# A two-layer conv / mLSTM / MLA block: 512-wide merges and a separate pool replaced by whole rows in generic slots, psum banks for the last chunk, and modulation pulled later

## The chip, the cores and the metric

The kernel runs on one core of one Trainium2 chip. The metric is the device time of one execution in microseconds; what is compared is the median of several runs.

## The reference

Two layers work on a sequence of 512 tokens and a context of 256 tokens, both 1024 wide. In each layer a modulation vector is made from `c` and `c_ctx`, one big projection `w_in` makes the inputs of three branches and their gates, the gated sum of the branches is projected and normalized, and an MLP with a squared ReLU follows. Cut to that:

```
mod = silu(c) @ w_mod[l] + b_mod[l]                 # six vectors of 1024; the same for c_ctx
u = x * (1 + sc1) + sh1
a, qkv, o_pre, g_if, cq, ckv, kr, gates = split(u @ w_in + b_in)
y_conv = silu(layer_norm(depthwise_conv(glu(a)))) @ w_conv_out
y_ml   = (sigmoid(o_pre) * layer_norm(mlstm(qkv, g_if))) @ w_mlstm_out
y_mla  = attention(cq, ckv, kr) @ w_mla_out         # keys of sequence and context
g_a, g_b, g_c = split(sigmoid(gates))
y = (g_a*y_conv + g_b*y_ml + g_c*y_mla) @ w_out + b_out
x = layer_norm(alpha*x + g1*y)
x = layer_norm(alpha*x + g2*(square(relu((x*(1+sc2)+sh2) @ w1 + b1)) @ w2 + b2))
```

In the first layer (layer 0) all of this is done for the context too. In the second (layer 1) the context only feeds attention and the mLSTM state, and the result is the sequence's `x`.

## The kernel before, in words

**Number format and weights.** Activations stand feature by token: a tile holds 128 features (partitions) and up to 768 tokens, 512 of the sequence and 256 of the context (`n` is 768 in layer 0, 512 in the later parts of layer 1; `segs` are these two pieces). Every product is made by three matmuls (`mm3`, L270 to L273) from a high and a low part of each factor. A weight tile of 128x1024 comes by a DMA on SP's queue (`wr`, L260), ScalarE casts it to the high part `wh` (L266), and VectorE or GpSimd subtracts to get the low part `wl` (L267). Three tiles of each exist, and `wget` loads two tiles ahead. `split` (L277, L278) does the same for an activation.

**Order of work.** A scheduler lays down a fixed order for each engine, and each engine works through its own in order; every DMA is issued on SP's queue. Only TensorE's order in the first stage and in the last chunk of layer 0 is written by hand (`manual_schedule`). TensorE's results go to psum: two tiles `pg` of two banks each and four tiles `pt` of one bank each. A tile of the next block may only be started when the operation that reads its predecessor is done.

**Modulation.** `mod_pieces` (L155 to L185) is a generator: a group of eight loads `wm` (256 KB each), eight or sixteen multiplies on VectorE into `mda` (L164, L166), eight small matmuls (L174), a copy (L177), a transpose (L179) and an add. There are four groups for each half of a layer's vectors. `pull(k)` lets the generator take k steps; it is called from the gates, the merges and the MLP, so the calls decide where these instructions stand.

**Gates, merges, output projection.** `gate` (L770) is a 128-row block of `w_in`, a tanh (L773), and a store to `z_dram`; there are 24 (three branches b of eight row blocks mt), then four O gates (L804) that stay in memory. Between the gates VectorE does the depthwise taps (L505), and after the eleventh gate the conv branch's LayerNorm stands (statistics, transposes L343 on TensorE, `conv_emit`). Then for each of the four mLSTM heads `ht` is transposed, multiplied by its O gate (L831), scaled (L832) and split (L277, L278). `merge(0)` multiplies the conv branch with `w_co`: eight blocks of twelve matmuls (three times 4) for each piece of tokens, and for each piece the gate is loaded again (`mload`, L77), multiplied with the psum tile (`ml`, L816) and stored. `merge(1)` does that for the mLSTM with `w_mo` and adds the sum so far. The MLA merge (L1091 to L1103) multiplies by `w_ao`, adds, and splits the total into `zp` (L1100 on ScalarE, L1101 on VectorE), the input of `w_out`. `mload` has eight tiles of 128x512 of its own (pool `mw`).

**Rows of constants.** `RC` holds five 1024-wide vectors; they are transposed (L853), stored to `v_dram`, and read back spread over 128 partitions by `rowv` (L858) into a pool `row` of five 128x1024 tiles. They are used in the MLP on GpSimd (L1252 to L1262) and, in layer 0, in the last chunk (L1274).

**MLP and the last chunk.** The MLP has eight chunks (`NF`) of 512 hidden features. In each, four blocks by `w1`, a squared ReLU, and `second`, which multiplies by `w2` token tile by token tile, for each half `hf` of the 1024 features, with VectorE adding the psum tile to `acc` (L1244). In the last chunk TensorE's order is by hand: for the four token tiles of the sequence (`GX`), then the two of the context (`GC`), half 0 and half 1 of the products; VectorE multiplies by a constant row into `t` (L1274) and adds (L1275); after half 1 the token's LayerNorm follows. The four tiles of `second` stand in the two `pg` tiles, one bank each, for both halves. After the context's products the sequence tokens are transposed (`tok_back`, L1191) and `norm2` (L1284 to L1294) makes the next layer's input: `xn` for a store, `uh` on ScalarE, `uf` on VectorE and `ul` on GpSimd, on VectorE for two of eight blocks.

**Pools.** Generic slots `gen` (128x768) 33; weights three each of `wr`, `wh`, `wl`; `mw` eight; `row` five.

Of the kernel before, what the change touches and what calls it, by code (L numbers as in the profile page):

```python
# [9 lines left out]
F32 = mybir.dt.float32  # L10
# [34 lines left out]
def build(tc, I, out):  # L45
    nc = tc.nc
# [1 line left out]
    ctx = ExitStack()  # L48
    cp = ctx.enter_context(tc.tile_pool(name="const", bufs=1))
    wp = ctx.enter_context(tc.tile_pool(name="w", bufs=3))  # L50
    gp = ctx.enter_context(tc.tile_pool(name="gen", bufs=33))
    vp = ctx.enter_context(tc.tile_pool(name="v", bufs=12))
    mp = ctx.enter_context(tc.tile_pool(name="mw", bufs=8))
    sp = ctx.enter_context(tc.tile_pool(name="small", bufs=6))
    pp = ctx.enter_context(tc.tile_pool(name="psum", bufs=1, space=bass.MemoryType.PSUM))
    rp = ctx.enter_context(tc.tile_pool(name="row", bufs=5))
    dp = ctx.enter_context(tc.tile_pool(name="dram", bufs=1, space=bass.MemoryType.DRAM))

    def slot(name, dt=F32):
# [13 lines left out]

    def mload(src):
        n = src.shape[1]
        t = mp.tile([128, 512], F32, name="ml", tag="m")
        nc.sync.dma_start(t[:, :n], src)  # L77
        return t[:, :n]

# [273 lines left out]
    def pull(k):  # L353
        for _ in range(k):
            next(mods, None)
# [108 lines left out]
    for l in range(L):  # L464
# [324 lines left out]
        for b in range(3):  # L789
            for mt in range(8):  # L790
                g = gate(b, mt)
                nc.sync.dma_start(z_dram[b, mt, :, :n], g[:, :n])
                some_taps(3)
                pull(2)
                if b * 8 + mt == 10:
                    some_taps(200)
                    ln_fm(ca, 4, groups, conv_emit)
# [3 lines left out]
        for h in range(MH):  # L801
            ps = win(MT_O + h, n)
            t = slot("ot")
            A.activation(t[:, :n], ps[:, :n], AF.Tanh, bias=HB(MT_O + h), scale=0.5)  # L804
            ot.append(t)
            pull(2)

        def merge(b, wname, act):
            for mp2 in range(4):
                w = wget(wname, l, mp2)  # L810
                for i in range(2):
                    mt = 2 * mp2 + i
                    ps = gemm(w, 4 * i, 4, act, n)
                    for c0, c1 in segs:
                        g = mload(z_dram[b, mt, :, c0:c1])
                        V.scalar_tensor_tensor(g, g, 1.0, ps[:, c0:c1], op0=OP.add, op1=OP.mult)  # L816
                        if b:
                            z0 = mload(z_dram[b - 1, mt, :, c0:c1])
                            G.tensor_tensor(g, g, z0, op=OP.add)
                        nc.sync.dma_start(z_dram[b, mt, :, c0:c1], g)  # L820
                    pull(2)


# [32 lines left out]
        nc.sync.dma_start(v_dram[l].rearrange("r (k j) -> (r k) j", j=128), rct[:40, :128])  # L856

        def rowv(i):  # L858
            t = rp.tile([128, 1024], F32, name="row", tag="row")
            nc.sync.dma_start(t, v_dram[l, i:i + 1, :].to_broadcast([128, 1024]))  # L860
            return t


        def latent(mt0, nt, gname, nn, scale):
# [225 lines left out]
        for mp2 in range(4):  # L1090
            w = wget("w_ao", l, mp2)  # L1091
            for i in range(2):
                mt = 2 * mp2 + i
                ps = gemm(w, 4 * i, 4, oT, n)
                for (_, _, c0, c1), zz in zip(tg_, zg):
                    g = mload(z_dram[2, mt, :, c0:c1])
                    z0 = mload(z_dram[1, mt, :, c0:c1])
                    V.scalar_tensor_tensor(g, g, 1.0, ps[:, c0:c1], op0=OP.add, op1=OP.mult)
                    V.tensor_tensor(g, g, z0, op=OP.add)
                    A.copy(zz[mt][0], g)  # L1100
                    V.tensor_sub(zz[mt][1], g, zz[mt][0])  # L1101

        u2 = [None] * 8  # L1103

# [92 lines left out]
        def second(f, hf, tts, wide):  # L1197

            ws = [None, None]
            sums = banks(len(tts), True) if wide else None  # L1200
            for i, tt in enumerate(tts):
                ps = sums[i] if wide else pt()
                for kp in range(2):
                    if not i:
                        ws[kp] = wget("w2", l, f, hf * 2 + kp)
                    tok_mm(ps, tt, hf, ws[kp], h_of, 2 * kp, 4)
                yield tt, ps
# [2 lines left out]
        b2r = [rowv(2 + v) for v in range(nv)]  # L1210
        g2r = [rowv(v) for v in range(nv)]
        if not full:
            folded.update({("w2", l, NF - 1, 2 * hf + kp): (g2r[0][:, hf * 512:hf * 512 + 512],)
                           for hf in range(2) for kp in range(2)})
        for f in range(NF):
            hid = []
            for j in range(FB):
                mt = f * FB + j
                last = j == FB - 1
                parts_f = split_spec if mt < 2 or last else [(c0, c1, c0) for c0, c1 in segs]  # L1220
                w = wget("w1", l, mt)
                if last:
                    sums = gemm_parts(w, 8, u2, parts_f)
                else:
                    sums = [(0, n, gemm(w, 0, 8, u2, parts_f)[:, :n])]
                r, hh, hl = slot("r"), slot("hidh", F32R), slot("hidl", F32R)
                for c0, c1, ps in sums:
                    A.activation(r[:, c0:c1], ps, AF.Relu, bias=col(l, "b1", mt))
                    A.activation(hh[:, c0:c1], r[:, c0:c1], AF.Square)
                    V.tensor_tensor(r[:, c0:c1], r[:, c0:c1], r[:, c0:c1], op=OP.mult)  # L1230
                    V.tensor_sub(hl[:, c0:c1], r[:, c0:c1], hh[:, c0:c1])  # L1231
                pull(1)
                hid.append((hh, hl))
            def h_of(k, tt):
                return hid[k][0][:, tt * 128:tt * 128 + 128], hid[k][1][:, tt * 128:tt * 128 + 128]

            if f < NF - 1:
                for hf in range(2):
                    for tt, ps in second(f, hf, qts, False):
                        if f == 0:  # L1240
                            acc[tt, hf] = vt512("acc")
                            A.copy(acc[tt, hf], ps)
                        else:
                            V.tensor_tensor(acc[tt, hf], acc[tt, hf], ps, op=OP.add)  # L1244
                        if tt % 3 == 2:
                            pull(1)
            if 1 <= f <= 6:
                for tt, hf in [(tt, hf) for tt in qts for hf in range(2)][2 * (f - 1):2 * f]:
                    r = wtile("r2")
                    o = hf * 512  # L1250
                    nc.sync.dma_start(r, n_dram[tt, hf])
                    G.tensor_tensor(r, r, a2r[:, o:o + 512], op=OP.mult)  # L1252
                    G.tensor_tensor(r, r, b2r[kind(tt)][:, o:o + 512], op=OP.add)
                    nc.sync.dma_start(r_dram[tt, hf], r)
            if f == 6:
                for hf in range(2):
                    for tt in qts:
                        o = hf * 512
                        r = wtile("r2")
                        nc.sync.dma_start(r, r_dram[tt, hf])  # L1260
                        G.tensor_tensor(acc[tt, hf], acc[tt, hf], g2r[kind(tt)][:, o:o + 512], op=OP.mult)
                        G.tensor_tensor(acc[tt, hf], acc[tt, hf], r, op=OP.add)  # L1262
        pull(99)
        if full:
# [2 lines left out]


        def last_w2(tts, hf):
            for tt, ps in second(NF - 1, hf, tts, True):  # L1270
                t = ps
                if full:
                    t = wtile("t2")
                    V.tensor_tensor(t, ps, g2r[kind(tt)][:, hf * 512:hf * 512 + 512], op=OP.mult)  # L1274
                V.tensor_tensor(acc[tt, hf], acc[tt, hf], t, op=OP.add)  # L1275
                tok_stats(tt, hf, acc[tt, hf])
                if hf:
                    yield tt

        if full:  # L1280
            u = [None] * 8

            def norm2(k, c0, c1, ps):
                v = 0 if c0 < S else 1  # L1284
                if c0 == 0:
                    u[k] = (slot("uh", F32R), slot("ul", F32R))
                if v == 0:
                    xn = wtile("xn")
                    A.activation(xn[:, :c1 - c0], ps, AF.Identity, bias=col(l, "ln2_b", k), scale=col(l, "ln2_g", k))
                    nc.sync.dma_start(xs_dram[k, :, c0:c1], xn[:, :c1 - c0])  # L1290
                uf = slot("uf")
                A.activation(u[k][0][:, c0:c1], ps, AF.Identity, bias=nq_[:, k, v:v + 1], scale=np_[:, k, v:v + 1])  # L1292
                V.tensor_scalar(uf[:, c0:c1], ps, np_[:, k, v:v + 1], nq_[:, k, v:v + 1], op0=OP.mult, op1=OP.add)
                (V if k % 4 == 3 else G).tensor_sub(u[k][1][:, c0:c1], uf[:, c0:c1], u[k][0][:, c0:c1])  # L1294

            with tc.manual_schedule(engines={mybir.EngineType.PE}):
                for gi, tts in enumerate((GX, GC)):
# [125 lines left out]
```

## Time and profile before

| | |
|---|---|
| median of 3 runs | 2570.15 us (2569.47 to 2571.76) |
| the profiled execution | 2566.69 us, of which the span of the trace is 2564.9 us |
| mean granted TensorE clock | 0.989 |
| TensorE (PE) busy | 2463.4 us, 96% of the span, 14618 matmuls |
| weight loads (PEld) busy | 2130.0 us, 83%, beside the matmuls |
| VectorE (DVE) busy | 1586.3 us, 62% |
| ScalarE (ACT) busy | 928.5 us, 36% |
| GpSimd (POOL) busy | 419.7 us, 16% |
| moved by DMA | 319.40 MB |

A row of a timeline gives the start in us from the span's start, the duration, the engine, the line, the operation, output<-inputs, the shape, and how many such instructions stand in a row; the bracket behind it says how long the engine was idle before it and what ended that. In the row of a group the times of all its instructions are added. In the list of DMA issues the last number is the median time from issue to landing.

### The profile page before, as it was taken

The page shows a single profiled execution, that of the slowest core. Times are in us where ns is not written, and L with a number is a line of the kernel's source. Part 1 is how long each engine was busy: PE and PEld are TensorE (multiplying, and loading weights), DVE is VectorE, ACT ScalarE, POOL GpSimd, SP SyncE. Part 2 cuts the span into 40 slices and gives each one's busy share as a digit, 9 for nine tenths or more (in the row PEclk, how much of TensorE's full clock was granted, in tenths as well). Part 3 has the DMA queues.
Part 4 walks back from the last instruction along what each step waited for, and adds up shares of the span by engine and source line. Part 5 has one row for each costly group of instructions (what it writes and reads, how often), then busy time and mean ns, then how long its engine had stood idle before and what let it go on. Part 6 is the DMA issues. An engine that isn't in the chain of part 4 may idle for free.

```text
span 2564.9 us, 37165 instructions
## 1 busy us (share of the span) xinstructions
PE 2463.4 (96%) x14618; PEld 2130.0 (83%) x14618; DVE 1586.3 (62%) x2795; ACT 928.5 (36%) x1577; POOL 419.7 (16%) x319
## 2 busy tenths in 40 slices
PE   7899989999999999999999979999999999999997
PEld 5888868888887898888888858978888889888886
DVE  4999976363356776655555379996043567544447
ACT  3123323222457553222222243333324575432322
POOL 0002132202000030010011520024421001500025
PEclk9999999999999999999999999999999999999999
DMA  7122344567110664444444232233563107633332
GB/s 263 53 75 69 101 159 160 172 198 241 62 33 5 195 204 144 128 145 139 147 131 140 80 97 82 65 107 97 177 211 127 50 18 230 206 98 91 106 91 83
DMA packets 148852, 319.40 MB, mean 125 GB/s; under 512 B 15076, under 2 KB 56628, under 8 KB 148676
## 3 DMA queue, kind: packets, MB, share of 16 engines
q1 hardware_dynamic: 148676, 317.02, 38.5%
q8 instruction: 115, 1.88, 0.3%
q14 instruction: 61, 0.50, 0.1%
HBM read 275.97 MB, written 40.98 MB: 124 GB/s over the span
## 4 chain that ended last, share of the span: by engine, by line
PE 50%; DVE 7%; issue 2%; ACT 2%; POOL 1%; DMA 0%; POOLq 0%; DVEq 0%; ACTq 0%
PE pg L271 8%; PE pg L272 8%; PE pg L273 8%; PE pt L272 6%; PE pt L273 6%; PE pt L271 6%; DVE ca L505 2%; DVE wl L267 1%; PE pt L1040 1%; PE pt L1019 1%; ACT wh L266 1%; PE pg L549 0%; PE pg L551 0%; PE pg L550 0%; DVE r L1230 0%
## 5 line engine op out<-in xcount | busy, mean ns | idle before, releaser
L266 ACT CAST wh<-wr 128x1024 fp32r<-128x1024 f32 (+2 forms) x320 | 337.6, 1056 | 1137.0 <-PE pg L272 493.1
L267 DVE TENSOR_TENSOR wl<-wr,wh 128x1024 fp32r<-128x1024 f32 (+1 forms) x264 | 344.8, 1307 | 448.0 <-ACT wh L266 447.2
L271 PE MATMUL pg<-uh,wh 128*128 128x512 f32 (+1 forms) x1280 | 456.9, 357 | 3.0 <-ACT uh L1292 1.8
L273 PE MATMUL pg<-uh,wl 128*128 128x512 f32 (+1 forms) x1280 | 454.9, 355 | 2.2 <-DVE wl L267 2.2
L272 PE MATMUL pg<-ul,wh 128*128 128x512 f32 (+1 forms) x1280 | 454.9, 355 | 0.6 <-POOL ul L1294 0.6
L271 PEld LDWEIGHTS pg<-uh,wh 128*128 128x128 f32 x1280 | 243.8, 191 | 38.3 <-issue 2.5
L273 PEld LDWEIGHTS pg<-uh,wl 128*128 128x128 f32 x1280 | 243.6, 190 | 34.9 <-DVE wl L267 2.7
L272 PEld LDWEIGHTS pg<-ul,wh 128*128 128x128 f32 x1280 | 244.0, 191 | 33.4 <-POOL ul L1294 1.6
L267 POOL TENSOR_TENSOR wl<-wr,wh 128x1024 fp32r<-128x1024 f32 x56 | 146.7, 2619 | 537.3 <-ACT wh L266 537.3
L505 DVE SCALAR_TENSOR_TENSOR ca<-hc,cols,ca 128x511 f32<-128x511 f32 (+9 forms) x360 | 227.1, 671 | 2.3
L273 PE MATMUL pt<-wh,hidl 128*128 128x512 f32 x560 | 218.7, 391 | 1.8 <-DVE hidl L1231 1.8
L272 PE MATMUL pt<-wl,hidh 128*128 128x512 f32 x560 | 219.0, 391 | 0.6 <-DVE wl L267 0.6
L271 PE MATMUL pt<-wh,hidh 128*128 128x512 f32 x560 | 218.4, 392 | 0.0
L272 PE MATMUL pg<-u2l,wh 128*128 128x512 f32 (+1 forms) x608 | 211.3, 348 | 0.6 <-POOL u2l L1112 0.2
L271 PE MATMUL pg<-u2h,wh 128*128 128x512 f32 (+1 forms) x608 | 210.4, 347 | 0.0
L273 PE MATMUL pg<-u2h,wl 128*128 128x512 f32 (+1 forms) x608 | 209.9, 346 | 0.0
L166 DVE SCALAR_TENSOR_TENSOR mda<-wm,sil,mda 128x512 f32<-128x512 f32 x224 | 180.0, 824 | 6.9 <-DMA wm<-w_mod 4.2
L1244 DVE TENSOR_TENSOR acc<-acc,pt 128x512 f32<-128x512 f32 x120 | 82.1, 684 | 123.0 <-PE pt L273 122.8
L272 PEld LDWEIGHTS pg<-u2l,wh 128*128 128x128 f32 x608 | 115.2, 189 | 17.1 <-POOL u2l L1112 2.6
L271 PEld LDWEIGHTS pg<-u2h,wh 128*128 128x128 f32 x608 | 115.0, 189 | 15.3 <-issue 1.2
L273 PEld LDWEIGHTS pg<-u2h,wl 128*128 128x128 f32 x608 | 115.0, 189 | 14.0
L273 PEld LDWEIGHTS pt<-wh,hidl 128*128 128x128 f32 x560 | 105.6, 188 | 24.7 <-DVE hidl L1231 2.6
(387 smaller groups left out, 4908.1 us busy)
## 6 DMA issues: line engine op xcount, KB each, us to landing
wr<-w SPq DMA_DIRECT2D x132, 512.0 KB, 3.5
wr<-w_in_fm SPq DMA_DIRECT2D x104, 512.0 KB, 3.6
wm<-w_mod SPq DMA_DIRECT2D x192, 256.0 KB, 4.3
wr<-w_out SPq DMA_DIRECT2D x40, 512.0 KB, 4.2
ml<-z_dram SPq DMA_DIRECT2D x104, 128.0 KB, 2.7
ml<-z_dram SPq DMA_DIRECT2D x48, 256.0 KB, 4.2
z_dram<-ml SPq DMA_DIRECT2D x32, 256.0 KB, 3.4
dm<-m_dram SPq DMA_DIRECT2D x20, 256.0 KB, 4.4
```

The source lines that it names most:

```text
L166: ins = V.scalar_tensor_tensor(av[v], w, sil[:, k, v:v + 1], av[v], op0=OP.mult, op1=OP.add)
L266: A.copy(h[:, :n], r[:, :n])
L267: eng.tensor_sub(lo[:, :n], r[:, :n], h[:, :n])
L271: PE.matmul(ps, hs, xh, start=first, stop=False)
L272: PE.matmul(ps, hs, xl, start=False, stop=False)
L273: return PE.matmul(ps, ls, xh, start=False, stop=last)
L505: V.scalar_tensor_tensor(acc[:, a:b], h[:, a + d:b + d], wd(15 + d), acc[:, a:b], op0=OP.mult, op1=OP.add)
L1019: PE.transpose(p2[:, y * 128:(y + 1) * 128], P[:, (k4 + y) * 128:(k4 + y + 1) * 128], ident)
L1040: PE.matmul(po[64 * i:64 * i + 64, :256], va[B_.k0 + k][:, h * 64:h * 64 + 64], B_.pts[i][k // 2][:, k % 2, :], start=(k == 0), stop=(k == ...
L1244: V.tensor_tensor(acc[tt, hf], acc[tt, hf], ps, op=OP.add)
```

## The change

1. The pool `gen` grows from 33 to 40 slots. The pool `row` goes: `rowv` now loads each row as two halves of 512 into generic slots. The loads of `mload` take a generic slot too; the pool `mw` is kept.
2. The gates call `pull(3)`, but only for the second and third branch (from the ninth gate on), where all called `pull(2)`; the O gates call `pull(3)`.
3. The merges work on whole rows of `n` tokens: one load, one multiply, one add, one store for a row block where layer 0 had two of each. In the MLA merge the total is split by groups afterwards.
4. In the last chunk `second` takes banks by `wide`: half 0 of the four sequence tokens in the two `pg` tiles as before, half 1 in the four `pt` tiles; the two context tokens stay in `pg`. Before, all stood in `pg`. In the second layer the same holds for its four tokens.
5. In `norm2` the last subtract is always on GpSimd.

The core of the diff:

```diff
-    gp = ctx.enter_context(tc.tile_pool(name="gen", bufs=33))
+    gp = ctx.enter_context(tc.tile_pool(name="gen", bufs=40))
-    rp = ctx.enter_context(tc.tile_pool(name="row", bufs=5))
...
-        t = mp.tile([128, 512], F32, name="ml", tag="m")
+        t = slot("ml")
...
-                pull(2)
+                if b:
+                    pull(3)
...
             ot.append(t)
-            pull(2)
+            pull(3)
...
                     ps = gemm(w, 4 * i, 4, act, n)
-                    for c0, c1 in segs:
-                        g = mload(z_dram[b, mt, :, c0:c1])
-                        V.scalar_tensor_tensor(g, g, 1.0, ps[:, c0:c1], op0=OP.add, op1=OP.mult)
-                        if b:
-                            z0 = mload(z_dram[b - 1, mt, :, c0:c1])
-                            G.tensor_tensor(g, g, z0, op=OP.add)
-                        nc.sync.dma_start(z_dram[b, mt, :, c0:c1], g)
+                    g = mload(z_dram[b, mt, :, :n])
+                    V.scalar_tensor_tensor(g, g, 1.0, ps[:, :n], op0=OP.add, op1=OP.mult)
+                    if b:
+                        z0 = mload(z_dram[b - 1, mt, :, :n])
+                        G.tensor_tensor(g, g, z0, op=OP.add)
+                    nc.sync.dma_start(z_dram[b, mt, :, :n], g)
...
-            t = rp.tile([128, 1024], F32, name="row", tag="row")
-            nc.sync.dma_start(t, v_dram[l, i:i + 1, :].to_broadcast([128, 1024]))
-            return t
+            ts = [slot("row")[:, :512] for _ in range(2)]
+            for hf, t in enumerate(ts):
+                nc.sync.dma_start(t, v_dram[l, i:i + 1, hf * 512:hf * 512 + 512].to_broadcast([128, 512]))
+            return ts
...
                 ps = gemm(w, 4 * i, 4, oT, n)
+                g = mload(z_dram[2, mt, :, :n])
+                z0 = mload(z_dram[1, mt, :, :n])
+                V.scalar_tensor_tensor(g, g, 1.0, ps[:, :n], op0=OP.add, op1=OP.mult)
+                V.tensor_tensor(g, g, z0, op=OP.add)
                 for (_, _, c0, c1), zz in zip(tg_, zg):
-                    g = mload(z_dram[2, mt, :, c0:c1])
-                    z0 = mload(z_dram[1, mt, :, c0:c1])
-                    V.scalar_tensor_tensor(g, g, 1.0, ps[:, c0:c1], op0=OP.add, op1=OP.mult)
-                    V.tensor_tensor(g, g, z0, op=OP.add)
-                    A.copy(zz[mt][0], g)
-                    V.tensor_sub(zz[mt][1], g, zz[mt][0])
+                    A.copy(zz[mt][0], g[:, c0:c1])
+                    V.tensor_sub(zz[mt][1], g[:, c0:c1], zz[mt][0])
...
-            sums = banks(len(tts), True) if wide else None
+            sums = banks(len(tts), wide) if f == NF - 1 else None
...
-            for tt, ps in second(NF - 1, hf, tts, True):
+            for tt, ps in second(NF - 1, hf, tts, len(tts) == 2 or not hf):
...
-                (V if k % 4 == 3 else G).tensor_sub(u[k][1][:, c0:c1], uf[:, c0:c1], u[k][0][:, c0:c1])
+                G.tensor_sub(u[k][1][:, c0:c1], uf[:, c0:c1], u[k][0][:, c0:c1])
```

The edits move instructions in the order of the engines. Three places follow, each as it stood before and as it stands now; after the change the lines of the helpers and of the gates and merges have a number lower by one (L174 becomes L173, L267 L266, L278 L277, L816 L815, L831 L830, L832 L831).

**TensorE, gates of layer 0.** Here is the first group of modulation matmuls (`mda`, L174) in TensorE's order. Before, it stands in a gate's block (`pg<-uh,wh`), some three gates ahead of the conv's LayerNorm:

```order
L271 MATMUL pg<-uh,wh 128x512
L272 MATMUL pg<-ul,wh 128x512
L174 MATMUL pt<-mda,pick 32x128 x4
L273 MATMUL pg<-uh,wl 128x512
L174 MATMUL pt<-mda,pick 32x128 x4
L271 MATMUL pg<-uh,wh 128x512
L272 MATMUL pg<-ul,wh 128x512
L179 MATMUL pt<-cst,modrows 128x128
L273 MATMUL pg<-uh,wl 128x512
```

Now it stands in the last gate ahead of the LayerNorm's transposes (`cst,ca`, L318):

```order
L270 MATMUL pg<-uh,wh 128x512
L271 MATMUL pg<-ul,wh 128x512
L173 MATMUL pt<-mda,pick 32x128 x8
L272 MATMUL pg<-uh,wl 128x512
L270 MATMUL pg<-uh,wh 128x512
L178 MATMUL pt<-cst,modrows 128x128
L318 MATMUL pt<-cst,ca 128x128 x16
```

All eight matmuls (L173) now stand together, and 16 transposes follow at the end of the same gate.

**VectorE, the start of the conv merge in layer 1.** `ht` is the mLSTM head's output, `htl` its low part, `ml` the merge's row, `wl` the low part of a merge's weights. Before, the merge's multiplies (L816) alternate with the heads:

```order
L816 SCALAR_TENSOR_TENSOR ml<-ml,pg 128x512
L267 TENSOR_TENSOR wl<-wr,wh 128x1024
L278 TENSOR_TENSOR htl<-ht,hth 128x512
L831 SCALAR_TENSOR_TENSOR ht<-ot,pt 128x512
L816 SCALAR_TENSOR_TENSOR ml<-ml,pg 128x512
L832 TENSOR_SCALAR ht<-ht,cols_86 128x512
L278 TENSOR_TENSOR htl<-ht,hth 128x512
L831 SCALAR_TENSOR_TENSOR ht<-ot,pt 128x512
L816 SCALAR_TENSOR_TENSOR ml<-ml,pg 128x512
L832 TENSOR_SCALAR ht<-ht,cols_86 128x512
L267 TENSOR_TENSOR wl<-wr,wh 128x1024
```

Now the heads' operations come first, and four multiplies (L815) follow together:

```order
L266 TENSOR_TENSOR wl<-wr,wh 128x1024
L277 TENSOR_TENSOR htl<-ht,hth 128x512
L830 SCALAR_TENSOR_TENSOR ht<-ot,pt 128x512
L831 TENSOR_SCALAR ht<-ht,cols_83 128x512
L277 TENSOR_TENSOR htl<-ht,hth 128x512
L830 SCALAR_TENSOR_TENSOR ht<-ot,pt 128x512
L831 TENSOR_SCALAR ht<-ht,cols_83 128x512
L277 TENSOR_TENSOR htl<-ht,hth 128x512
L815 SCALAR_TENSOR_TENSOR ml<-ml,pg 128x512 x4
L266 TENSOR_TENSOR wl<-wr,wh 128x1024
```

The first L815 in this order now stands behind the last `htl` (L277).

**VectorE and SP, the MLA merge in layer 1.** On VectorE the multiply (L1098 before, L1097 now), the add (L1099, now L1098) and the split (L1101) of one row block, before in two halves of 256 tokens:

```order
L1098 SCALAR_TENSOR_TENSOR ml<-ml,pg 128x256
L267 TENSOR_TENSOR wl<-wr,wh 128x1024
L1101 TENSOR_TENSOR zp<-ml,zp 128x256
L1099 TENSOR_TENSOR ml<-ml 128x256
L1098 SCALAR_TENSOR_TENSOR ml<-ml,pg 128x256 x2
L1101 TENSOR_TENSOR zp<-ml,zp 128x256
L1099 TENSOR_TENSOR ml<-ml 128x256 x2
L1101 TENSOR_TENSOR zp<-ml,zp 128x256
L1098 SCALAR_TENSOR_TENSOR ml<-ml,pg 128x256
L1101 TENSOR_TENSOR zp<-ml,zp 128x256
L267 TENSOR_TENSOR wl<-wr,wh 128x1024
```

and now in one of 512:

```order
L266 TENSOR_TENSOR wl<-wr,wh 128x1024
L1097 SCALAR_TENSOR_TENSOR ml<-ml,pg 128x512
L1098 TENSOR_TENSOR ml<-ml 128x512
L1097 SCALAR_TENSOR_TENSOR ml<-ml,pg 128x512
L1101 TENSOR_TENSOR zp<-ml,zp 128x256 x2
L1098 TENSOR_TENSOR ml<-ml 128x512
L1101 TENSOR_TENSOR zp<-ml,zp 128x256 x2
L1097 SCALAR_TENSOR_TENSOR ml<-ml,pg 128x512
L1098 TENSOR_TENSOR ml<-ml 128x512
L266 TENSOR_TENSOR wl<-wr,wh 128x1024
```

The low part of the weights (`wl`) now stands ahead of two multiplies in a row of L1097 and L1098, where halves of L1098 and L1101 stood around it. On SP's queue, before, the loads of the gates' rows (L77) stand in halves between the loads of the weights (L260):

```order
L77 DMA ml<-z_dram 128x256 x14
L260 DMA wr<-w_out 128x1024
L77 DMA ml<-z_dram 128x256 x7
L260 DMA wr<-w_out 128x1024
L77 DMA ml<-z_dram 128x256 x8
L260 DMA wr<-w_out 128x1024
L77 DMA ml<-z_dram 128x256 x3
L1120 DMA xr<-xs_dram 128x2x256 x4
L260 DMA wr<-w_out 128x1024
```

and now in whole rows (L76) between the weights (L259), with the loads of the block input (`xr`) further ahead:

```order
L76 DMA ml<-z_dram 128x512 x2
L1120 DMA xr<-xs_dram 128x2x256 x3
L76 DMA ml<-z_dram 128x512 x2
L259 DMA wr<-w_out 128x1024
L76 DMA ml<-z_dram 128x512 x4
L259 DMA wr<-w_out 128x1024
L76 DMA ml<-z_dram 128x512 x2
L259 DMA wr<-w_out 128x1024
L76 DMA ml<-z_dram 128x512 x6
L259 DMA wr<-w_out 128x1024 x9
```

There are 32 loads of halves in the stretch shown before, and 16 of whole rows now.

More of the change, by code (lines that the diff above doesn't have):

```diff
@@ L1199, in second @@
             ws = [None, None]
-            sums = banks(len(tts), True) if wide else None
+            sums = banks(len(tts), wide) if f == NF - 1 else None
             for i, tt in enumerate(tts):
-                ps = sums[i] if wide else pt()
+                ps = sums[i] if sums else pt()
                 for kp in range(2):
@@ L1212, in build @@
         if not full:
-            folded.update({("w2", l, NF - 1, 2 * hf + kp): (g2r[0][:, hf * 512:hf * 512 + 512],)
+            folded.update({("w2", l, NF - 1, 2 * hf + kp): (g2r[0][hf],)
                            for hf in range(2) for kp in range(2)})
@@ L1251, in build @@
                     nc.sync.dma_start(r, n_dram[tt, hf])
-                    G.tensor_tensor(r, r, a2r[:, o:o + 512], op=OP.mult)
-                    G.tensor_tensor(r, r, b2r[kind(tt)][:, o:o + 512], op=OP.add)
+                    G.tensor_tensor(r, r, a2r[hf], op=OP.mult)
+                    G.tensor_tensor(r, r, b2r[kind(tt)][hf], op=OP.add)
                     nc.sync.dma_start(r_dram[tt, hf], r)
@@ L1260, in build @@
                         nc.sync.dma_start(r, r_dram[tt, hf])
-                        G.tensor_tensor(acc[tt, hf], acc[tt, hf], g2r[kind(tt)][:, o:o + 512], op=OP.mult)
+                        G.tensor_tensor(acc[tt, hf], acc[tt, hf], g2r[kind(tt)][hf], op=OP.mult)
                         G.tensor_tensor(acc[tt, hf], acc[tt, hf], r, op=OP.add)
@@ L1273, in last_w2 @@
                     t = wtile("t2")
-                    V.tensor_tensor(t, ps, g2r[kind(tt)][:, hf * 512:hf * 512 + 512], op=OP.mult)
+                    V.tensor_tensor(t, ps, g2r[kind(tt)][hf], op=OP.mult)
                 V.tensor_tensor(acc[tt, hf], acc[tt, hf], t, op=OP.add)
```

## The prediction

> **What bounds the kernel now.** I read the page first, then what TensorE (PE) waited for over the whole run, then the table of windows for the clock, then the timelines around the places that the diff touches. The page shows one engine that is nearly always busy:
>
> ```profile
> span 2564.9 us, 37165 instructions
> PE 2463.4 (96%) x14618; PEld 2130.0 (83%) x14618; DVE 1586.3 (62%) x2795; ACT 928.5 (36%) x1577; POOL 419.7 (16%) x319
> ```
>
> PE is idle for about 101 us. The change adds and removes no matmul, so it can only move PE's waits and its clock. The list of PE's waits (total, times, longest, in us) has these that stand where the diff is:
>
> ```profile
> PE pt L174 <- DVE mda L166: 9.7, 2, 8.0
> PE pg L271 <- DVE t L1274: 7.1, 6, 2.0
> PE pt L343 <- ACT ln L331: 6.0, 9, 2.2
> PE pt L1191 <- DVE uf L1293: 5.0, 3, 2.8
> PE pg L271 <- DVE acc L1275: 3.6, 2, 3.0
> PE pg L271 <- DVE ml L816: 1.7, 1, 1.7
> PE pg L271 <- DVE ml L1098: 1.0, 2, 0.8
> ```
>
> The merges (L816, L1098) cost almost nothing now. A wait also has a second price, in the table of windows of 3.41 us (length, PE busy, granted clock):
>
> ```profile
> 331.50:334.94 3.44, 0.00 (x0) 1.00 0.65 251
> 338.35:341.77 3.42, 3.42 (x19) 0.50 0.81 244
> ...
> 1502.30:1505.71 3.41, 1.44 (x8) 1.00 0.52 159
> 1505.71:1509.12 3.41, 3.41 (x8) 0.50 0.39 149
> ```
>
> After 1.97 us of idleness in one window, the next window, fully busy, was granted 0.50: a loss of half of it, 1.7 us. The Trainium skill (TensorE: Matmul & The Clock Gate, HAM oscillation — how this bites in real kernels) asks only that no gap be longer than about 3.4 us; the trace disagrees, with 1.97. By that rule the clock costs that I add to the two output-projection merges (3.6 in all) would be nil and the 1.7 won back in the last chunk too, and the sum 1.9 lower.
>
> **Gates of layer 0.**
>
> ```profile
> 337.78 0.66 PE L174 MATMUL pt<-mda,pick 128*32 128x128 f32 x8 [7.98 <-DVE mda L166]
> ...
> 331.69 6.70 DVE L166 SCALAR_TENSOR_TENSOR mda<-wm,sil,mda 128x512 f32<-128x512 f32 x10
> ...
> 374.37 2.93 DVE L166 SCALAR_TENSOR_TENSOR mda<-wm,sil,mda 128x512 f32<-128x512 f32 x1
> ...
> wm<-w_mod SPq DMA_DIRECT2D x192, 256.0 KB, 4.3
> ```
>
> The first modulation group now stands directly ahead of the conv's LayerNorm transposes, some three gates later. The 7.98 us go, and with them the half clock from 337.78 to 341.77 (half of 4.0, 2.0 us). The multiply that took 2.93 us between the LayerNorm's statistics stands no longer there, so most of the 2.2 us wait on L331 goes: 2.0. What is late next: the sixteen multiplies need eight loads, five of which stand on SP behind the store of the ninth gate. From that store PE has two gates of 8.34 us (spacing of the casts below) to go; loads 4.3, five issues and the last two multiplies make about 7.5. No wait. The second group keeps a wait of 1.7 (14 multiplies instead of 4 are left when the LayerNorm is done, 6.7 us more, but PE comes about 7 us later). Sum -12.0; bounds -8 (LayerNorm waits stay, 2 us for late loads) and -14.
>
> **Last chunk of layer 0.**
>
> ```profile
> 1490.82 0.50 PE L271 MATMUL pg<-wh,hidh 128*128 128x512 f32 x1 [1.25 <-DVE t L1274]
> 1497.93 0.50 PE L271 MATMUL pg<-wh,hidh 128*128 128x512 f32 x1 [1.37 <-DVE t L1274]
> ...
> 1505.64 0.76 PE L271 MATMUL pg<-wh,hidh 128*128 128x512 f32 x1 [1.97 <-DVE t L1274]
> ```
>
> The second half of the four sequence tokens gets four single banks, so the first two waits (2.6) go. The third was for tiles held by that half; about 1.0 stays between the halves of one tile, 1.0 goes, and the half-clock window after it, 1.7. PE then reaches the transposes L1191 3.6 us earlier and waits there for the same `uf`: I let 1.0 be lost, moving the last `ul` to GpSimd included. Sum -4.3; bounds -1 and -9 (the half-clock windows there go too).
>
> **Merge of the conv branch, layer 1.** New: all DVE work on `ht` stands ahead of the first L815, the operation that frees a psum tile, where it alternated before. PE has two tiles, so the third block waits.
>
> ```profile
> 1883.27 0.69 DVE L816 SCALAR_TENSOR_TENSOR ml<-ml,pg 128x512 f32<-128x512 f32 x1 [0.19 <-PE pg L273]
> 1886.89 1.23 DVE L267 TENSOR_TENSOR wl<-wr,wh 128x1024 fp32r<-128x1024 f32 x1 [0.22 <-ACT wh L266]
> 1888.03 0.69 DVE L278 TENSOR_TENSOR htl<-ht,hth 128x512 fp32r<-128x512 f32 x1
> 1888.63 0.68 DVE L831 SCALAR_TENSOR_TENSOR ht<-ot,pt 128x512 f32<-128x512 f32 x1
> 1889.83 0.48 DVE L832 TENSOR_SCALAR ht<-ht,cols 128x512 f32<-128x512 f32 x1
> ...
> 1880.36 1.05 ACT L266 CAST wh<-wr 128x1024 fp32r<-128x1024 f32 x1 [3.80 <-issue]
> 1885.80 1.05 ACT L266 CAST wh<-wr 128x1024 fp32r<-128x1024 f32 x1 [2.08 <-PE pg L272]
> 1890.40 0.62 ACT L277 CAST hth<-ht 128x512 fp32r<-128x512 f32 x1 [3.02 <-DVE ht L832]
> ```
>
> Both casts at 1880.36 and 1885.80 start as PE frees weights: two blocks take 5.44 us. At 1885.8 the second is done, and the third needs L815, which stands behind this chain from 1888.03: `htl` 0.60, `ht` 0.60 and 0.48, `hth` 0.62, `htl` 0.60, again 0.60, 0.48, 0.62, 0.60, then L815 0.69 and some hand-offs: 1894.1. PE is ready at 1886.2, after the row transpose that now comes first: it waits 7.9, bounds 6 and 9. Clock afterwards 1.7 (0.8 to 2.6, by where the restart falls in a window). Sum +9.6.
>
> **The same, layer 0.**
>
> ```profile
> 530.86 1.05 ACT L266 CAST wh<-wr 128x1024 fp32r<-128x1024 f32 x1 [6.49 <-issue]
> 542.65 1.05 ACT L266 CAST wh<-wr 128x1024 fp32r<-128x1024 f32 x1
> ...
> 531.38 1.02 DVE L831 SCALAR_TENSOR_TENSOR ht<-ot,pt 128x512 f32<-128x512 f32 x2 [5.10 <-PE pt L829]
> 533.45 0.61 DVE L832 TENSOR_SCALAR ht<-ht,cols 128x768 f32<-128x768 f32 x1
> 534.96 0.96 DVE L278 TENSOR_TENSOR htl<-ht,hth 128x768 fp32r<-128x768 f32 x1 [0.90 <-ACT hth L277]
> ...
> 534.10 0.83 ACT L277 CAST hth<-ht 128x768 fp32r<-128x768 f32 x1 [1.38 <-DVE ht L832]
> ...
> ml<-z_dram SPq DMA_DIRECT2D x48, 256.0 KB, 4.2
> ```
>
> Let the last gate end at 0. Two blocks end at 11.0 (542.65 less 530.86, less 0.9 for modulation matmuls that move behind them). DVE does four heads (pair 0.94, 0.53, 0.88 each at the pace of back-to-back rows, plus waits for `hth` 0.83), six multiplies of 0.67 and two `wl`: the third `wl`, which waits for the cast at 11.0, ends at 13.7, the last `htl` at 17.9. Only behind that `wl` SP issues the next weights and the first z row; it lands 4.2 later, at about 18.1. L815, whole row, 0.96 by the `htl` row: PE starts at 19.0, having done 1.2 us of small work since 11.0. It waits 6.8, in place of 1.7; clock 1.7. Sum +6.8, bounds +4 and +9.
>
> **Output-projection merges.**
>
> ```profile
> 887.60 0.39 PE L273 MATMUL pg<-zp,wl 128*128 128x256 f32 x1 [0.75 <-DVE wl L267]
> 2137.09 0.47 PE L271 MATMUL pg<-zp,wh 128*128 128x256 f32 x2 [0.83 <-DVE ml L1098]
> 2115.85 0.76 DVE L1101 TENSOR_TENSOR zp<-ml,zp 128x256 fp32r<-128x256 f32 x2
> ```
>
> Whole rows leave no half to slip in between. Layer 1, block 2.72 long: `wl` now stands ahead of the L1097 of an older block, and needs the cast that PE's previous block releases: 1.05 + 1.14 + 0.69 gives 2.8 at the fifth block, and with an L1101 pair but a block's time of cover 0.7 at the fourth. For the eighth, the z row stands on SP behind the weights that wait for that `wl`: 2.2 + 0.5 + 4.2 (3.0 if it lands like a short one) + 0.6, less 2.72: 3.5. At the end 0.5. Sum 7.5 against 1.0, +6.4, and 2.4 of clock (two waits, 0.7 x 1.7 each): +8.8, bounds +3 and +13. Layer 0, block 4.17: only the eighth: 2.2 + 0.5 + 4.2 + 0.9 less 4.17 is 3.6, less 0.75: +2.9, clock 1.2: +4.1, bounds 0 and +8.
>
> **Tail.**
>
> ```profile
> 2548.40 0.55 POOL L1173 TENSOR_TENSOR rs<-rs,mhalf 128x1 f32<-128x1 f32 x1
> 2553.47 0.55 POOL L1173 TENSOR_TENSOR rs<-rs,mhalf 128x1 f32<-128x1 f32 x1
> ```
>
> The wait of 3.0 on L1275 goes, but GpSimd paces the four tokens (5.07 from one to the next, busy throughout but for 1.12), starting from the first token, which is not earlier. Worth 0, bounds -2 and +1. Row halves in generic slots: loaded long before use, 0; without that cover, one landing of 4.2.
>
> **Rivals.** *Deep enough everywhere (faster).* More buffers end bubbles: all waits of L1274 and L1191 (12.1) and the half clock go in the last chunk, some -16.7, and z rows come ahead of need, so that L1097 never waits: -12.0 - 16.7 + 6.8 + 9.6 = -12.3, 2558. The Trainium skill (Perfetto Trace Analysis, Optimization Strategy) reads repeated bubbles as too few buffers, which is this case. It decides if `uf` is done within 1.8 us of PE's asking. Against it: the `uf` chain is DVE time, not banks. *Only the merge starts bite.* z rows land in time and `wl` slips in: -12.0 - 4.3 + 6.8 + 9.6 = 0.1, 2570. Decided by landing within 2 us. *Modulation late:* if the five loads come 11 us later than I reckon, 12.0 is lost: 2595.
>
> **How the numbers follow.** Sum: -12.0 - 4.3 + 9.6 + 6.8 + 8.8 + 4.1 + 0 = +13.0. The profiled run took 2566.69, 3.5 below the median of 2570.15; I set the sum on the median: 2583. Chances: forecast 0.65, deep enough 0.15, starts only 0.15, late modulation 0.05. The forecast's own bounds, not all at once, give 2575 to 2593; down to 2566 takes in the second rival. A measurement tells 0.2% (5 us) from no change: faster 0.15, same 0.15, slower 0.70.
>
> **What would show it.** Right: L173 without a wait near 365; a PE wait of 6 to 9 us on L815 at the third block of both conv merges, with a 0.50 window behind it; waits on L1097. Wrong: L815 of the first block running before the last `htl`, no L1097 in the list of PE's waits, or a wait on `mda` of several us.

## The result, and the profile after

The changed kernel takes 2590.11 us in the median of 4 runs (2588.26 to 2590.64), the kernel before 2569.81 beside it: a ratio of 1.0078, with a 95% interval of 1.006 to 1.0095. It is 20 us slower. 13 were forecast, with a range that holds the result.

First the head of the page of the changed kernel, then the list of TensorE's waits (total, times, longest, in us), cut to the places of the diff:

```profile
span 2586.5 us, 36902 instructions
PE 2469.6 (95%) x14618; PEld 2136.0 (83%) x14618; DVE 1579.8 (61%) x2725; ACT 926.3 (36%) x1577; POOL 419.6 (16%) x317
```

```profile
PE pg L270 <- DVE ml L1097: 13.5, 6, 4.8
PE pg L270 <- DVE ml L815: 10.5, 2, 8.3
PE pt L173 <- DVE mda L165: 5.8, 2, 4.2
PE pt L1191 <- DVE uf L1293: 5.1, 4, 2.1
PE pg L270 <- DVE t L1274: 3.3, 4, 0.9
PE pt L852 <- DVE rc L849: 2.6, 1, 2.6
PE pt L342 <- ACT ln L330: 2.2, 6, 0.5
...
PE pt L342 <- DVE rs L326: 1.7, 1, 1.7
```

Of the 21.6 us by which the span grew, TensorE's busy time has 6.2 (2469.6 less 2463.4), with the same 14618 matmuls: that is the clock. In windows of 3.41 us over the whole trace, 24 were granted 0.50 here and 16 before, with 56.5 and 40.9 us of TensorE's work in them. The other 15.4 are idle time. The multiplies of the merges (L815, L1097), which held TensorE up for 2.7 us in all, now do so for 24.0. The waits on `mda`, `t` and `ln` became shorter, as forecast.

TensorE's timeline shows where. The bracket holds the idle time before the row:

```profile
406.02 0.43 PE L173 MATMUL pt<-mda,pick 128*32 128x128 f32 x8 [4.19 <-DVE mda L165]
...
536.18 0.65 PE L173 MATMUL pt<-mda,pick 128*32 128x128 f32 x16 [1.57 <-DVE mda L165]
537.25 0.33 PE L178 MATMUL pt<-cst,modrows 128*128 128x128 f32 x1 [0.43 <-ACT modrows L176]
540.13 0.37 PE L852 MATMUL pt<-cst,rc 128*40 128x128 f32 x1 [2.55 <-DVE rc L849]
542.75 0.79 PE L270 MATMUL pg<-sah,wh 128*128 128x512 f32 x1 [2.24 <-DVE ml L815]
...
876.65 0.47 PE L270 MATMUL pg<-oh,wh 128*128 128x512 f32 x1 [3.77 <-DVE ml L1097]
885.29 0.38 PE L271 MATMUL pg<-zp,wh 128*128 128x256 f32 x1 [0.38 <-DVE zp L1101]
886.92 0.36 PE L270 MATMUL pg<-zp,wh 128*128 128x256 f32 x1 [1.12 <-DVE ml L1097]
...
1896.92 0.79 PE L270 MATMUL pg<-sah,wh 128*128 128x512 f32 x1 [8.29 <-DVE ml L815]
...
2134.15 0.50 PE L270 MATMUL pg<-oh,wh 128*128 128x512 f32 x1 [0.73 <-DVE ml L1097]
...
2139.93 0.50 PE L270 MATMUL pg<-oh,wh 128*128 128x512 f32 x1 [2.77 <-DVE ml L1097]
2154.80 0.80 PE L270 MATMUL pg<-oh,wh 128*128 128x512 f32 x1 [4.78 <-DVE ml L1097]
```

The start of the conv merge (`sah`) waits 8.29 in layer 1; in layer 0 four waits of 6.8 in all stand ahead of the same place. The MLA merge (`oh`) waits in both layers. The table of windows (length, TensorE busy, granted clock, share of DMA, GB/s) shows what comes on top:

```profile
539.96:546.78 6.82, 4.41 (x11) 0.50 1.01 372
871.06:874.47 3.41, 1.82 (x14) 1.00 0.74 233
874.47:877.88 3.41, 1.23 (x5) 1.00 1.03 380
877.88:881.29 3.41, 3.41 (x10) 0.50 0.60 237
884.70:888.12 3.42, 1.92 (x14) 1.00 0.52 153
888.12:891.53 3.41, 3.41 (x18) 0.50 0.00 0
1891.63:1901.87 10.24, 4.95 (x12) 0.50 0.92 313
2140.81:2144.22 3.41, 3.41 (x10) 0.50 0.76 284
2154.46:2157.87 3.41, 3.07 (x7) 0.50 0.71 260
```

At each of these places but the wait of 0.73 (2134.15) a window is granted 0.50, behind the wait or around its end. Half of the busy time in the rows at 0.50, 22.66 us, is 11.3 lost; the kernel before had such windows at other places, so TensorE's busy time grew by less.

### The profile page after: what moved, and what is told of

The parts are those of the page before. It is cut to its first block, busy times and chain, and to the rows that moved or that the text cites. A ratio compares the mean times of both kernels' runs of the same rounds, so it can differ in the third digit from the quotient of the medians.

```text
span 2586.5 us, 36902 instructions
## 1 busy us (share of the span) xinstructions
PE 2469.6 (95%) x14618; PEld 2136.0 (83%) x14618; DVE 1579.8 (61%) x2725; ACT 926.3 (36%) x1577; POOL 419.6 (16%) x317
## 5 line engine op out<-in xcount | busy, mean ns | idle before, releaser
L266 DVE TENSOR_TENSOR wl<-wr,wh 128x1024 fp32r<-128x1024 f32 (+1 forms) x264 | 341.8, 1295 | 461.1 <-ACT wh L265 459.3
L271 PE MATMUL pt<-wl,hidh 128*128 128x512 f32 x592 | 230.8, 390 | 0.6 <-DVE wl L266 0.6
L266 POOL TENSOR_TENSOR wl<-wr,wh 128x1024 fp32r<-128x1024 f32 x56 | 142.6, 2546 | 543.7 <-ACT wh L265 531.0
L272 PE MATMUL pt<-wh,hidl 128*128 128x512 f32 x592 | 230.2, 389 | 0.0
L270 PE MATMUL pt<-wh,hidh 128*128 128x512 f32 x592 | 229.9, 390 | 0.0
L271 PEld LDWEIGHTS pt<-wl,hidh 128*128 128x128 f32 x592 | 111.2, 188 | 24.1 <-DVE wl L266 1.8
L272 PEld LDWEIGHTS pt<-wh,hidl 128*128 128x128 f32 x592 | 111.2, 188 | 23.1
L270 PEld LDWEIGHTS pt<-wh,hidh 128*128 128x128 f32 x592 | 111.5, 188 | 22.6
```

The source lines that it names most:

```text
L266: eng.tensor_sub(lo[:, :n], r[:, :n], h[:, :n])
L270: PE.matmul(ps, hs, xh, start=first, stop=False)
L271: PE.matmul(ps, hs, xl, start=False, stop=False)
L272: return PE.matmul(ps, ls, xh, start=False, stop=last)
```

## The experiments

**Theories.** Theory A: the merges' rows are late since they are loaded into generic slots, which other tiles hold, so that their loads stand late on SP and their multiplies late on VectorE. Theory B, the one in the prediction for the output merges: whole rows leave no half to slip in between. In order of time the changed kernel's SP queue has this around the conv merge of layer 1 and in the MLA merge:

```profile
1890.71 0.34 SPq L259 DMA_DIRECT2D wr<-w_mo  x1
1891.13 2.29 SPq L76 DMA_DIRECT2D ml<-z_dram  x5
...
2149.45 0.33 SPq L259 DMA_DIRECT2D wr<-w_out  x1
2149.83 2.80 SPq L76 DMA_DIRECT2D ml<-z_dram  x6
```

The conv merge's five first rows are asked for at 1891.13, after TensorE has begun to wait (1888.63).

**A pool of their own.** The first two runs separate the pool from the width.

```diff
-        t = slot("ml")
+        t = mp.tile([128, 768], F32, name="ml", tag="m")    # pool of six; gen 39
```

> The changed kernel with one thing undone: the merges' rows come from a pool of their own (six tiles of 128x768, gen 39 slots), still as whole rows. Theory A, the generic slots are what costs (a row's load stands late on SP and late in VectorE's order): in the conv merge of layer 1 the first multiply stands behind the first head again and the wait of 8.3 us is gone, in layer 0 about half of 8, and most of the 9.4 and 5.3 us of waits in the output merges go with their clock: 2560, between 2554 and 2567. Theory B, whole rows are what costs (nothing to slip in between): only layer 1's conv merge gets better, where a row was whole before too, by 10.7: 2579. If neither holds: 2590.

Measured: 2551.41 us (2547.04 to 2554.16), against before 0.9932, interval 0.9919 to 0.9944. It is 39 us faster than the changed kernel, more than theory A asked for, and 18 faster than the kernel before. Its SP queue at the same places:

```profile
1781.29 3.40 SPq L76 DMA_DIRECT2D ml<-z_dram  x5
...
2091.25 15.44 SPq L76 DMA_DIRECT2D ml<-z_dram  x9
2107.51 0.33 SPq L259 DMA_DIRECT2D wr<-w_out  x1
```

Here the five rows are asked for some 90 us ahead of their use, and nine rows of the MLA merge stand ahead of the third tile of `w_out`, where the changed kernel has four. On VectorE the first multiply of the conv merge stands ahead of the first head's `htl` again; the changed kernel has it behind the fourth, and it starts there as soon as VectorE is free (1896.19). First the run with the own pool, then the changed kernel:

```profile
1870.29 0.69 DVE L815 SCALAR_TENSOR_TENSOR ml<-ml,pg 128x512 f32<-128x512 f32 x1 [0.19 <-PE pg L272]
1870.90 0.69 DVE L277 TENSOR_TENSOR htl<-ht,hth 128x512 fp32r<-128x512 f32 x1
```

```profile
1895.58 0.69 DVE L277 TENSOR_TENSOR htl<-ht,hth 128x512 fp32r<-128x512 f32 x1 [0.69 <-ACT hth L276]
1896.19 1.27 DVE L815 SCALAR_TENSOR_TENSOR ml<-ml,pg 128x512 f32<-128x512 f32 x2
```

The second run also puts the old merges back, by pieces, in eight tiles of 128x512 of their own.

> The changed kernel with the merges as before: rows by pieces from a pool of their own of eight tiles of 128x512 (gen 39). Theory A: within 4 us of e1_own_pool, since whole rows as such cost nothing. Theory B: 2560, and lower than e1_own_pool by 15 or more.

Measured: 2555.46 us (2548.45 to 2558.83), 0.9944 (0.9931 to 0.9957). Pieces in place of whole rows are not faster, and the intervals of the two overlap. Theory B falls: whole rows cost nothing.

**Slots alone, with pieces.** The kernel before, with gen 40, constant rows in slots, and `mload` taking slots.

> The kernel before with only the storage changed: 40 generic slots, constant rows in slots, the merges' loads in slots; merges by pieces, pulls and banks as before. Theory A: the start of both conv merges has all head work ahead of the first multiply, +10.7 in layer 1 and 4 to 9 in layer 0, and some of the output merges' waits: 2588, between 2582 and 2597. Theory B: +10.7 at most, 2580 or less, with no waits on the multiplies of the output merges.

Measured: 2636.41 us, 1.0267 (1.0253 to 1.0281), 67 us slower than before, far above what theory A gave. Its waits on the merges' multiplies (the MLA merge's is L1098 here), then the only such row of the run with the own pool:

```profile
PE pg L270 <- DVE ml L1098: 29.1, 10, 6.9
PE pg L270 <- DVE ml L815: 19.1, 2, 10.8
```

```profile
PE pg L270 <- DVE ml L815: 1.0, 2, 0.8
```

Loading into slots is the fault, and pieces make it worse: each takes a whole slot, so where a row is loaded in two pieces there are twice as many late loads. This run lacks the pulls and banks too, so the price of the slots is taken between runs that differ in little else: 72 us for pieces (under "The storage" below), the 39 above for whole rows. Whole rows soften the damage of the slots; the prediction had it the other way round.

**Which merges.** The own pool for the conv and mLSTM merges, slots for the two rows of the MLA merge.

```diff
-    def mload(src):
+    def mload(src, own=True):
-        t = mp.tile([128, 768], F32, name="ml", tag="m")
+        t = mp.tile([128, 768], F32, name="ml", tag="m") if own else slot("ml")
...
-                g = mload(z_dram[2, mt, :, :n])
+                g = mload(z_dram[2, mt, :, :n], False)          # z0 the same
```

> e1_own_pool with only the two rows of the output merges (w_ao) loaded into generic slots again; the conv and mLSTM merges keep their own pool. If the costs of the late rows add up by place, this gives back what stands there in the changed kernel's trace, 7 in layer 0 and 10 to 12 in layer 1: 2569, between 2565 and 2573, with waits on L1097 of about 5 and 8 us in all and none on L815. If the output merges only pay for the late start of the conv merges: 2553.

Measured: 2570.94 us (2567.37 to 2577.32), 1.0015 (1.0006 to 1.0024).

```profile
PE pg L270 <- DVE ml L1097: 12.9, 6, 5.0
...
PE pg L270 <- DVE ml L815: 0.2, 1, 0.2
```

The MLA merges keep their six waits and the conv merges lose theirs. The costs add up by place: 19.5 for the MLA merges (2570.94 less 2551.41), 19.2 for the other two (2590.11 less 2570.94). The kernel before took 2567.47 beside this run, 2569.47 beside the own pool and 2569.81 beside the changed kernel; set against these, the two parts are 21.5 and 16.8, so each is known to some 2 us.

**Fewer slots.** The changed kernel with gen 37.

> The changed kernel with 37 generic slots in place of 40. Theory A1, the merges' rows suffer because they are given slots that other tiles hold until the last O gates, three slots more or less being no matter: 2590, within 3. Theory A2, there are simply too few slots: 2600 or more.

Measured: 2589.06 us (2583.61 to 2590.97), 1.0074 (1.0062 to 1.0086). Three slots less change nothing, which speaks for A1. Which tiles held the slots is read from the changed kernel's program. In both layers the eight rows of the conv merge take over the slots of the four O gates (`ot`) and the four heads' outputs (`ht`), whose last readers are L830 and L277 on VectorE. So each of these loads has to come behind a step of the heads' work, and the multiplies with them. The rows of the MLA merges take over slots of the attention's tiles, which, but for one, TensorE reads last.

**The gains: pulls and banks.** First both on the kernel before.

> The kernel before with two edits alone: the pulls from the ninth gate on, and the single banks for the second half of the last chunk. By the shift of TensorE's matmuls between the two traces (9 us earlier after the gates of layer 0, 5.5 us earlier after the last chunk) the time is 2555, between 2551 and 2560. Rival: the later modulation group and the constant rows give it back where the merge of layer 0 starts (waits of 4.2, 1.7 and 2.6 us stand there in the changed kernel): 2562 to 2566.

Measured: 2561.65 us (2559.78 to 2564.01), 0.9971 (0.9961 to 0.9981): 7.8 faster, where some 14.5 were expected. The time is near the rival's, but not for its reason: of the waits that it names the 4.2 on `mda` stands in this run, but the 2.6 on `rc` does not. Then each is taken out of the own-pool version.

> e1_own_pool with the pulls as before. If the pulls are worth what TensorE's shift in layer 0 shows (about 8 us by the LayerNorm's end, after their own waits of 4.3 and 1.8): 2559, between 2556 and 2563, with the wait of some 8 us on the first modulation group back. If the later modulation is only a wait at another place: within 2 us of e1_own_pool.

Measured: 2560.91 us (2554.98 to 2565.12), 0.9966 (0.9955 to 0.9977). The pulls are worth 9.5. The wait on the first modulation group is back:

```profile
340.98 0.66 PE L173 MATMUL pt<-mda,pick 128*32 128x128 f32 x8 [8.01 <-DVE mda L165]
```

> e1_own_pool with both halves of the last chunk in the two wide tiles as before the change. The banks are worth the 4.5 us by which TensorE gets ahead in the last chunk of layer 0 between the traces, and nothing in the tail, where GpSimd paces: 2556, between 2554 and 2559, with the wait of 3.0 on the last acc back and the end no later for it. Rival, the uf chain takes the gain back: 2552.

Measured: 2556.42 us (2555.31 to 2559.1), 0.9958 (0.9944 to 0.9971). The banks are worth 5.0, or 7.0 when each run is set against the kernel before beside it (2567.47 and 2569.47). The two worths make 14.5 to 16.5 from this base, and 7.8 from the kernel before; the difference was not run down, beyond the next run. The edit of `norm2` was not tried by itself.

**The storage.** The kernel before with gen 40 and the constant rows in slots, the merges' pool kept.

> The kernel before with 40 generic slots and the constant rows in slots, and nothing else: merges, their own pool, pulls, banks and norm2 as before. As predicted, the rows are loaded long before use and the edit costs nothing: 2569, within 2. Rival: more slots are worth something by themselves, since in the runs with own pool the wait of 1.8 us on hidl at the first MLP chunk of layer 1 is gone with the clock behind it (3.5 in all) and small waits elsewhere: 2564, between 2562 and 2566.

Measured: 2564.05 us (2562.07 to 2568.63), 0.9986 (0.9977 to 0.9995): 4.3 faster. The rival holds: the wait of 1.8 us on `hidl` (L1231) is no longer in its list of waits. From e4_slots_only this run differs only in the pool of the merges' loads, so for pieces the slots cost 72 us (2636.41 less 2564.05).

**The second modulation group.** Its wait (4.2 in the changed kernel) was to be made smaller, first by no pulls in the two gates beside the LayerNorm, then by two in place of three in three gates.

```diff
-                    pull(3)
+                    pull(3 if mt < 3 and b == 1 else 0 if b * 8 + mt < 13 else 4)     # first
+                    pull(2 if 10 < b * 8 + mt < 14 else 3)                             # second
```

> e1_own_pool with the pulls resting in the two gates beside the LayerNorm (3 a gate for the ninth to eleventh, none for two gates, then 4 a gate). If the wait of 4.3 us on the second group comes from its multiplies standing behind the LayerNorm on VectorE, it goes or shrinks below 1 us, with its clock: 2546, between 2543 and 2550. Rival: the group is late wherever it is pulled, because its loads are late on SP: 2551.

> e1_own_pool with 2 pulls in place of 3 in the three gates at the LayerNorm. If VectorE's share of those gates decides, the wait of 4.3 us on the second group shrinks to 1 to 3: 2549, between 2546 and 2552. If its loads and multiplies are simply one group's 13 us behind the LayerNorm, TensorE waits as long as before: 2551.

Measured: 2560.01 us (2557.64 to 2562.46), 0.9964 (0.9952 to 0.9976), and 2558.22 us (2554.99 to 2559.31), 0.9962 (0.9949 to 0.9974). Both lose most of what the pulls gave. The wait in the first run, in the second, and in the own-pool version:

```profile
417.36 1.08 PE L173 MATMUL pt<-mda,pick 128*32 128x128 f32 x16 [6.02 <-DVE mda L165]
```

```profile
413.09 1.08 PE L173 MATMUL pt<-mda,pick 128*32 128x128 f32 x16 [5.76 <-DVE mda L165]
```

```profile
411.50 0.42 PE L173 MATMUL pt<-mda,pick 128*32 128x128 f32 x8 [4.25 <-DVE mda L165]
```

The wait did not shrink. That it grew by the edit is not shown: e10_own_no_banks, with the pulls of the own-pool version, waits 5.77 there. Behind this group the second run is hardly later than the own-pool version, whose other eight matmuls follow at 412.67. It loses at the conv merge of layer 0, where L815 makes TensorE wait 2.2 us in place of 0.2, with more multiplies of the modulation standing between its own. The first run waits on later groups as well, 11.8 us on `mda` in three waits with this one. In the own-pool version VectorE and SP have this ahead of it:

```profile
400.61 11.51 DVE L165 SCALAR_TENSOR_TENSOR mda<-wm,sil,mda 128x512 f32<-128x512 f32 x14 [2.17 <-DMA wm<-w_mod]
```

```profile
397.35 8.49 SPq L160 DMA_DIRECT2D wm<-w_mod  x6
```

The group's loads start at 397.35, when the LayerNorm is nearly done, and 14 multiplies take 11.5 us. This is what both rivals say, though neither foresaw the loss: the wait is one group's work behind the LayerNorm, and fewer pulls there only push the rest of the modulation into the next stage.

**The tail.** 128 of 512 columns of the last scale and add (L1320, L1321), for three of the four tokens, go from GpSimd to VectorE.

> e1_own_pool with 128 of 512 columns of the last scale and add of three tokens moved from GpSimd to VectorE. If GpSimd paces the end (5.07 us from token to token), the spacing falls by two operations of 128 columns, 0.8, to 4.3, and three tokens later the end is 2.4 earlier: 2549. If TensorE or the psum tiles pace it, the spacing stays at 5.07 and the time at 2551.

Measured: 2554.39 us (2550.68 to 2555.74), 0.994 (0.9928 to 0.9952): no gain. GpSimd's first operation of a token (L1173) starts every 5.0 us in the own-pool version; with the columns moved it starts at 2529.66, 2534.60, 2539.92 and 2544.57, so still 5.0 apart on average, and it now waits for VectorE:

```profile
2532.64 0.55 POOL L1173 TENSOR_TENSOR rs<-rs,mhalf 128x1 f32<-128x1 f32 x1
...
2537.67 0.54 POOL L1173 TENSOR_TENSOR rs<-rs,mhalf 128x1 f32<-128x1 f32 x1
```

```profile
2529.66 0.99 POOL L1173 TENSOR_TENSOR rs<-rs,mhalf 128x1 f32<-128x1 f32 x1 [15.74 <-DVE rs L1172]
...
2534.60 0.99 POOL L1173 TENSOR_TENSOR rs<-rs,mhalf 128x1 f32<-128x1 f32 x1 [0.54 <-DVE rs L1172]
2536.71 1.18 POOL L1320 TENSOR_TENSOR acc<-acc,gb 128x384 f32<-128x384 f32 x1 [1.12 <-ACT acc L1315]
```

VectorE's part in that run, from its own timeline (a moved piece, then the last token's, which is twice as wide):

```profile
2536.96 1.08 DVE L1320 TENSOR_TENSOR acc<-acc,gb 128x128 f32<-128x128 f32 x1
...
2546.63 0.42 DVE L1320 TENSOR_TENSOR acc<-acc,gb 128x256 f32<-128x256 f32 x1 [0.22 <-ACT acc L1315]
```

The piece of 128 columns takes 1.08 and ends at 2538.04, just behind GpSimd's operation, which ran from 2536.71 to 2537.89; the piece of 256 that begins ahead of GpSimd's takes 0.42. All six moved pieces of this run end 0.14 to 0.16 us behind the GpSimd operation beside them. What is moved to VectorE waits for GpSimd all the same. The Trainium skill (Perfetto Trace Analysis, Optimizing Scalar/DVE Operations) says that the two share a read port of the memory, which a VectorE operation on two ports holds as an exclusive lock, so that moving work from one to the other might not help; this trace agrees, with 1.08 us for 128 columns. So the tail's spacing is GpSimd's and VectorE's together, and neither TensorE nor the psum tiles set it. In e10_own_no_banks, where TensorE waits 3.0 us for the last `acc` again, the four L1173 lie 15.2 us apart from first to last (2534.63 to 2549.87), and in the own-pool version 15.6 (2527.10 to 2542.70).

## Why the prediction was right, and where its sizes and one cause were off

The direction and most of the places were right, and the time is inside the range. That it lies there is partly luck: the merges cost 9 us more than reckoned, and the storage, put at nothing, gave 4 back. None of the rivals' times came. But one sign that the prediction had named for being wrong did, a wait on `mda` of several us. By parts, with the runs that price them:

| term | forecast, us | measured, us | from |
|---|---|---|---|
| gates and modulation | -12.0 | -9.5 | e1_own_pool less e5_own_no_pulls |
| last chunk (banks, norm2) | -4.3 | -5.0, banks alone | e1_own_pool less e10_own_no_banks |
| row halves, slots | 0 | -4.3 | e12_slots_rows less before |
| conv and mLSTM merges, both layers | +16.4 | +19.2 | changed kernel less e11_own_conv_only |
| MLA merges, both layers | +12.9 | +19.5 | e11_own_conv_only less e1_own_pool |
| sum | +13.0 | +19.9 | directly: +20.3 |

Each part is known to some 2 us, as said above.

**Gates.** The first group's wait went, as reckoned, and the LayerNorm's waits fell from 6.0 to 3.9. The second group waits 4.19, not 1.7, and the window behind it (406.84 to 410.25) runs at half clock. The reckoning had 14 multiplies follow the LayerNorm at once, at 0.67 each. In the changed kernel VectorE first waits 1.82 for their loads, which start at 390.92, 2.3 us ahead of the LayerNorm's end, and the 14 take 11.3 us, 0.8 each.

**Last chunk.** The waits on `t` fell from 7.1 to 3.3, and those on `uf` stayed (5.0, now 5.1). The term was right within what the runs resolve. In the tail the banks bring TensorE ahead, and the end is not earlier for it.

**Conv merges.** "All DVE work on `ht` stands ahead of the first L815" was the right step: 8.29 where 7.9 was reckoned. In layer 0 the 6.8 reckoned came to 6.8, but split over four waits, of which 2.24 is on L815, since the second modulation half and the constant rows stand there as well; that the sums agree so closely is luck. The rest is clock: in layer 1 4.95 us of work at half speed, 2.5 where 1.7 was put, and in layer 0 4.41, 2.2 where 1.7 was put.

**MLA merges.** The chain of `wl` ahead of an older L1097 and the row behind the weights on SP came as reckoned, with waits of 0.7, 2.8 and 4.8 in layer 1 against 0.7, 2.8 and 3.5. The 3.5 is a slip: its terms make 4.8 with the landing of 4.2, and 3.6 only with the 3.0 that stands in brackets; 4.8 was measured. In layer 0 "only the eighth" was right for the merge, 3.77 before the eighth block where 3.6 was reckoned. What it missed are 1.5 more at the start of `w_out`, and the clock: both places have a window at half clock (3.41 us busy each, 3.4 lost), where 0.7 of one was counted. And the cause given, that whole rows leave no half to slip in, is the step that failed. With the own pool, whole rows on L1097 are not in the list of waits; with slots, halves wait longer (29.1 in place of 13.5).

**Storage.** "Loaded long before use, 0" was right as far as the lists of waits show, and missed what more slots do elsewhere: the wait on `hidl`. The rival that put the time down to more buffers had that much in it.

Open: why pulls and banks together give 7.8 on the kernel before and 14.5 to 16.5 beside the own pool and more slots.

The best version is e1_own_pool, the change with six tiles of the merges' own: 2551.41 us, 0.9932 (0.9919 to 0.9944) of the kernel before.

## What to carry to other kernels

A small pool of its own lets a load be issued far ahead of its use; put into a large common pool, the same load gets its place when some long-lived tile goes, and in a queue that works in order the consumer and all that stands behind it go late with it. Look where the load stands on its queue, not only how many buffers there are: here 40 slots were worse than eight small tiles. And price a wait of some 2 us with a second price, the clock behind it; a shorter one may have it too.

## What the runs showed of the hardware

The clock can be halved behind less idle time than the 1.97 us of the prediction: in the window from 884.70, with the waits of 0.38 and 1.12 us, TensorE was idle for 1.50 us in all, and the next was granted 0.50. But the window from 871.06 had 1.59 us of idle time, and the next was granted 1.00. In the traces of both kernels, from 20 us on, every window of 3.41 us granted 1.00 in which TensorE was idle for 1.82 us or more was followed by one at 0.50; from 1.42 to 1.76 us both occur, and what decides there stays open. A wait of 8.29 us cost three windows (1891.63 to 1901.87), of which TensorE was busy for 4.95 us. And VectorE's 1.08 us for 128 columns beside GpSimd, against 0.42 for 256, was not expected of a move that takes work off the engine in the way.
